# Tile 0 in smaller pieces, Fourier copies on ScalarE, and four moved steps between the stages of a diffusion layer

## The chip, the cores and the metric

The kernel runs on one core of one Trainium2 chip. The metric is the device time of one execution, in microseconds (us). All work is in float32, with matmuls whose operands are split into a high and a low part.

## What is computed

One layer of a diffusion backbone for 256 context tokens and 2048 latent tokens, width 1024. Cut to what matters:

```python
sh1, sc1, g1, sh2, sc2, g2 = split(silu(c) @ w_mod + b_mod, 6)      # modulation vectors, c_ctx for context tokens
h = rms_norm(x, norm1_g) * (1 + sc1) + sh1
q, k, v, f = project(h, w_in)                                        # QK-norm; rotary embedding on latent tokens
attn = diff_attention(q, k_all, v_all, lam)                          # (softmax_0 - lam * softmax_1) @ v, 4 heads
four = real(fft2(f, axes=(positions, channels))) @ w_four            # 4 groups of 128 channels
x = x + g1 * (concat[rms_norm(attn, subln_g) * (1 - lam_init), four] @ w_out)
h = rms_norm(x, norm2_g) * (1 + sc2) + sh2
x = x + g2 * (square(relu(h @ w1)) @ w2)
```

Outputs are x of both groups and the new keys and values of the context tokens.

## The kernel before

There are 18 tiles of 128 tokens. The stages follow each other: modulation vectors and tile 0, projections of all tiles, Fourier mixing, attention (4 heads, latent tokens in groups), the output projection, then the two layers of the MLP, each as a Strassen-like scheme of seven products per block (p is the product's number). A split matmul is three: high x high, low x high, high x low (`mm3`, lines 94 to 96). Most of the order is written out by hand in `manual_schedule` blocks; in attention a list of events sorted by a number sets it. Tiles of pools with `reuse_waits="tile"` share memory with those of earlier stages: a write waits until whatever lay at the address before is no longer read.

**Start (lines 471 to 590).** The modulation row is summed in two ways. Columns for `pr` go through TensorE (line 484); the rest is multiplied by VectorE into two accumulators, macc_l and macc_h (line 490), which VectorE reduces across partitions (line 528, `sums`), so that TensorE spreads them with the constant matrix `quad` (line 537, `pm`). Then scale and shift are made (modc, scale), tile 0's normalised and transposed x becomes hTa, its high and low parts hh and hl (lines 555, 556), and TensorE starts the projections `pj`. The weights arrive as `win`; ScalarE makes the high part wh (line 513), VectorE the low part wl (line 516).

**Fourier (lines 746 to 779).** `yT` makes for each item py and pz on TensorE (lines 753, 755); ScalarE copies py to yu; VectorE writes the difference and the sum of yu and pz to ys (lines 767, 768). Items are 512, 256, 128 and 129 (HW) columns wide; for the 512 wide ones pz is copied as well and the sums are made later. The result of each channel group, ys0 to ys3, is stored to DRAM (`four`) by a DMA that GpSimd issues (line 829).

**Attention.** TensorE makes scores Ss (line 1080), VectorE their maximum mxs, ScalarE the exponential into P0s or P1s (line 1104), GpSimd combines both (lines 1119, 1120), TensorE transposes into pts (line 1135), ScalarE or VectorE copies that to ahs (line 1142), VectorE makes the low part als (line 1147), and TensorE multiplies with V into po (lines 94 to 96, 1161). The outcome of a group goes through o1 to o6: o1 copies it to oTs, o2 transposes it back (line 1176), o3 is the VectorE copy to os (line 1180).

**Output projection (lines 1540 to 1720).** `out_mm(i, hf)` is 24 matmuls of a tile's half into po, `out_post` adds it to x on VectorE, `x_norm` makes xn, and `finish(i)` transposes xn in eight matmuls into two PSUM tiles ptb (line 248) from which ScalarE makes hTb in eight copies (line 251). `mix` transposes am (line 1572).

**MLP.** `h_parts(b, p)` returns two steps: `high` is ScalarE's copy mhh (line 1479), `rest` VectorE's mhl (line 1483). The weight sums are VectorE's: `mlp_ahead(2)` (line 1515) and `w_add` (line 1719, ws); oplW is the low part of a weight (line 1451). Products go to the PSUM tiles pA to pD, and VectorE takes them out as u and uz (lines 1771 to 1781). The second layer, the y stage, writes to six rotating PSUM tiles ps.

Of the kernel before, what the change touches and what calls it, by code (L numbers as in the profile page):

```python
# [37 lines left out]
def f32(ap):  # L38
    return ap.bitcast(F32)


def body(tc, a, out):
    nc = tc.nc
    ctx = ExitStack()
    with ctx:
# [211 lines left out]
        with ExitStack() as c1:  # L257
# [206 lines left out]
            with tc.manual_schedule():  # L464
                with tc.tile_pool(name="p0r", bufs=3) as rows, tc.tile_pool(name="p0m", bufs=KD - 3, side="right") as more:
# [8 lines left out]
                    z = quads(t2, "quad0")  # L474
# [7 lines left out]
                    for k in range(KD):  # L482
                        for gi, w in enumerate((512, 512, 256)):
                            nc.tensor.matmul(pr[gi][0:2, :w], cols[:, k:k + 9:8], wm[k][:, gi * 512:gi * 512 + w], start=(k == 0), stop=(k == KD - 1))
                        for s in range(2):
# [7 lines left out]
                        if 3 <= k < 7:  # L493
                            for x in (2 * k - 6, 2 * k - 5):
                                nc.tensor.transpose(at0(x), X[0][:, x * P:(x + 1) * P], ident)
                    X.pop(0)
# [4 lines left out]
                with tc.tile_pool(name="p0h", bufs=6, reuse_waits="tile") as halves:  # L501
# [24 lines left out]
                    sums = t2("sums0")[:, 0:48].rearrange("p (s c) -> p s c", s=2)  # L526
                    for s in range(2):
                        nc.vector.tensor_reduce(sums[:, s, :], acc[s].rearrange("p (c i) -> p c i", i=32), axis=AX.X, op=ALU.add,
                                                apply_transpose=True)
                    for gi in range(3):  # L530
                        w = 256 if gi == 2 else 512
                        r = t2(f"mr{gi}")
                        nc.scalar.copy(r[0:2, :w], pr[gi][0:2, :w])
                        for j in range(w // P):
                            nc.tensor.transpose(pm[:, gi * 4 + j, :], r[0:2, j * P:(j + 1) * P], ident[0:2, 0:2])
                    for q in range(4):
                        nc.tensor.matmul(pq, z[:, 96 - 32 * q:224 - 32 * q], sums[:, :, q::4], start=(q == 0), stop=(q == 3))
                    for g in range(4):
                        w_high(0, g)
                    w_rest(0, 0)  # L540
                    nc.vector.tensor_add(modc[:, 0:10, :], pm, cols[:, 32:42].unsqueeze(2).to_broadcast([P, 10, 2]))
                    nc.vector.tensor_add(modc[:, 10:16, :], pq.rearrange("p s j -> p j s"), cols[:, 42:48].unsqueeze(2).to_broadcast([P, 6, 2]))
                    mk_scale(scale1, 8, 80)
# [3 lines left out]
                    def h_first(b):  # L547
                        for k in range(4 * b, 4 * b + 4):
                            sc, sh, dst = scale1[:, k, 1:2], modc[:, k, 1:2], h0[b][:, k % 4, :]
                            if k in (2, 3):  # L550
# [3 lines left out]
                        hi, lo = (x[:, b * 4:b * 4 + 4, :] for x in HH[0])  # L554
                        nc.vector.tensor_copy(hi, h0[b])  # L555
                        nc.vector.tensor_sub(lo, h0[b], f32(hi))
# [1575 lines left out]
```

## Time and profile before

| | before |
|---|---|
| median of 3 runs | 2862.53 us (2861.9 to 2864.64) |
| profiled execution | 2863.18 us, span 2861.4 us |
| granted TensorE clock | 0.999 on average |
| TensorE busy | 2831.7 us, 99% of the span |
| VectorE, ScalarE, GpSimd busy | 71%, 54%, 38% |

Times in the profile count from the start of the span. "[1.56 <-DVE xn L235]" behind an instruction says that its engine stood idle for 1.56 us before it and that VectorE's xn ended that. PE is TensorE, PEld its weight loads, DVE VectorE, ACT ScalarE, POOL GpSimd. A matmul's duration contains the drain of its pipeline; distances between starts tell the pace.

### The profile page before, as it was taken

To read this page: it belongs to the slowest core of one execution; us is meant where nothing else is said; L and a number is where in the kernel's file an instruction comes from. 1 tells how busy PE (TensorE), PEld (TensorE's weight loads), DVE (VectorE), ACT (ScalarE), POOL (GpSimd) and SP (SyncE) were. 2 spreads that over 40 slices of the span, in tenths; PEclk is the share of its full clock that TensorE was granted. 3 is DMA by queue.
4 is the path that set the end of the run, shared out by engine and by line. 5 is a ranking of instruction groups with operands and counts; after the bars stand their busy time and mean duration, and the time that the engine had idled before them with its cause. 6 is when DMAs were issued, how large, how long until landed. Compare 5 with 4: busy or idle time off the path is not lost.

```text
span 2861.4 us, 43224 instructions
## 1 busy us (share of the span) xinstructions
PE 2831.7 (99%) x15109; PEld 2455.9 (86%) x15109; DVE 2018.0 (71%) x3393; ACT 1548.2 (54%) x3505; POOL 1073.3 (38%) x890
## 2 busy tenths in 40 slices
PE   8999999999999999999999999999999999999999
PEld 5888888688888888888889999999998888888887
DVE  7767886898988989864477777778775354345554
ACT  4333323798989989853356565556555332333221
POOL 1211223798999989942223333333332000000000
PEclk9999999999999999999999999999999999999999
DMA  7776777421211212036767676667747464445663
GB/s 284 219 207 198 230 213 237 172 106 38 73 71 53 106 38 99 23 124 201 242 221 232 223 246 228 221 219 238 234 167 255 147 202 135 138 144 185 206 206 111
DMA packets 392780, 492.94 MB, mean 172 GB/s; under 512 B 26467, under 2 KB 306384, under 8 KB 389490
## 3 DMA queue, kind: packets, MB, share of 16 engines
q1 hardware_dynamic: 387136, 479.73, 50.9%
q0 software_dynamic: 1872, 7.28, 0.8%
q10 hardware_dynamic: 3554, 3.17, 0.4%
q8 instruction: 119, 1.95, 0.3%
q14 instruction: 99, 0.81, 0.1%
HBM read 312.58 MB, written 179.59 MB: 172 GB/s over the span
## 4 chain that ended last, share of the span: by engine, by line
PE 54%; DVE 1%; DMA 0%; ACT 0%; issue 0%; SPq 0%; POOL 0%; DVEq 0%; POOLq 0%
PE ps L94 8%; PE ps L95 8%; PE ps L96 8%; PE pB L1749 2%; PE pB L1747 2%; PE pB L1748 2%; PE pA L1748 2%; PE pC L1748 2%; PE pA L1749 2%; PE pC L1747 2%; PE pA L1747 2%; PE pC L1749 2%; PE po L94 2%; PE po L96 2%; PE po L95 2%; PE pD L1749 1%
## 5 line engine op out<-in xcount | busy, mean ns | idle before, releaser
L1085 DVE TENSOR_REDUCE mxs<-Ss 128x1 f32<-128x512 f32 x636 | 405.4, 686 | 65.5 <-PE Ss L1080 55.1
L1420 DVE TENSOR_TENSOR sl<-sr,sh 128x768 fp32r<-128x768 f32 x168 | 161.8, 964 | 331.5 <-ACT sh L1419 331.1
L1120 POOL TENSOR_TENSOR P0s<-P0s,P1s 128x1024 f32<-128x1024 f32 (+2 forms) x128 | 378.6, 2958 | 10.7
L1419 ACT CAST sh<-sr 128x768 fp32r<-128x768 f32 x168 | 140.6, 838 | 418.3 <-PE ps L95 418.3
L1789 POOL TENSOR_TENSOR gs<-g,g 128x384 f32<-128x384 f32 x48 | 69.7, 1452 | 468.5 <-ACT g L1759 418.9
L1104 ACT ACTIVATE P1s<-Ss,mxs 128x512 f32<-128x512 f32 x318 | 215.4, 694 | 36.3 <-DVE mxs L1088 35.3
L94 PE MATMUL pj<-wh,hh 128*128 128x512 f32 x576 | 228.8, 397 | 2.0 <-DVE hh L555 2.0
L94 PE MATMUL ps<-thT,sh 128*128 128x512 f32 x585 | 227.6, 389 | 0.0
L95 PE MATMUL ps<-tlT,sh 128*128 128x512 f32 x585 | 227.6, 389 | 0.0
L96 PE MATMUL ps<-thT,sl 128*128 128x512 f32 x585 | 227.6, 389 | 0.0
L95 PE MATMUL pj<-wl,hh 128*128 128x512 f32 x576 | 227.1, 394 | 0.5 <-DVE wl L516 0.5
L96 PE MATMUL pj<-wh,hl 128*128 128x512 f32 x576 | 225.6, 392 | 0.0
L1104 ACT ACTIVATE P0s<-Ss,mxs 128x512 f32<-128x512 f32 x318 | 214.3, 691 | 5.6 <-DVE mxs L1088 5.0
L1135 PE MATMUL pts<-ident,P0s 128*128 128x128 f32 x1280 | 191.7, 273 | 4.5 <-DVE als L1147 1.8
L1080 PE MATMUL Ss<-KS0s,Qs 128*128 128x512 f32 x636 | 190.1, 419 | 0.4 <-ACT P1s L1104 0.4
L1080 PE MATMUL Ss<-KS1s,Qs 128*128 128x512 f32 x636 | 188.7, 420 | 1.5 <-ACT P0s L1104 1.4
L1758 ACT ACTIVATE g<-uz 128x384 f32<-128x384 f32 x144 | 75.7, 526 | 200.2 <-DVE uz L1781 174.1
L1135 PEld LDWEIGHTS pts<-ident,P0s 128*128 128x128 f32 x1280 | 151.3, 140 | 35.9 <-issue 4.8
L1119 POOL TENSOR_SCALAR P1s<-P1s,tots 128x1024 f32<-128x1024 f32 (+2 forms) x128 | 171.9, 1343 | 5.8
L1147 DVE TENSOR_TENSOR als<-pts,ahs 128x512 fp32r<-128x512 f32 x256 | 165.9, 681 | 6.9 <-ACT ahs L1142 6.7
L94 PE MATMUL ps<-ophT,sh 128*128 128x512 f32 x423 | 164.7, 389 | 1.1 <-DVE uz L1781 1.1
L96 PE MATMUL ps<-ophT,sl 128*128 128x512 f32 x423 | 164.6, 389 | 0.0
(536 smaller groups left out, 8073.9 us busy)
## 6 DMA issues: line engine op xcount, KB each, us to landing
sr<-sd SPq DMA_DIRECT2D x84, 768.0 KB, 4.5
a<-in_w SPq DMA_DIRECT2D x184, 256.0 KB, 4.2
sd<-gs SPq DMA_DIRECT2D x192, 192.0 KB, 1.9
sd<-g SPq DMA_DIRECT2D x144, 192.0 KB, 2.1
wm<-in_w_mod SPq DMA_DIRECT2D x32, 512.0 KB, 5.2
Qs<-qd SPq DMA_DIRECT2D x32, 512.0 KB, 4.0
b<-in_w SPq DMA_DIRECT2D x64, 256.0 KB, 5.8
b<-tsum SPq DMA_DIRECT2D x64, 256.0 KB, 4.7
```

Source lines behind the costliest of these rows:

```text
L94: nc.tensor.matmul(ps, lh, rh, start=first, stop=False)
L95: nc.tensor.matmul(ps, lh, rl, start=False, stop=False)
L96: nc.tensor.matmul(ps, ll, rh, start=False, stop=last)
L1080: nc.tensor.matmul(S[:, :w], self.Q[:, x, m, j * P:j * P + P], self.hd.KS[m][:, b * 512:b * 512 + w], start=(x == 0), stop=(x == 1))
L1085: nc.vector.tensor_reduce(self.mx[j][:, m, b:b + 1], self.S[j, m, b], axis=AX.X, op=ALU.max)
L1104: nc.scalar.activation(dst, S, AF.Exp, bias=self.mx[j][:, m, 6:7], accum_out=self.sm[j][:, m, b:b + 1])
L1119: nc.gpsimd.tensor_scalar(p, p, tot[:, 3:4], 0.0, op0=ALU.mult, op1=ALU.add)
L1120: nc.gpsimd.tensor_add(d, d, p)
L1135: nc.tensor.transpose(pt[:, c:c + P], self.p0[j][:, (kb + t) * P:(kb + t + 1) * P], ident)
L1747: nc.tensor.matmul(ps, wh[:, c], hh[:, k, :], start=first and k == 0, stop=False, skip_group_check=True)
L1748: nc.tensor.matmul(ps, wh[:, c], hl[:, k, :], start=False, stop=False, skip_group_check=True)
L1749: nc.tensor.matmul(ps, wl[:, c], hh[:, k, :], start=False, stop=k == 3, skip_group_check=True)
```

## The change

Six edits at six places. Lines of the changed kernel lie 13 to 20 higher.

1. Start: `quad` and `sums` go. TensorE multiplies each 128-column piece of the accumulators with a column of ones (12 matmuls into `pm`), macc_l is finished first, two transposes of x move behind, scale is made in two parts, and hh and hl of tile 0 in three pieces (columns 0 to 1, 2 to 3, 4 to 7); two of the weights' parts move ahead of modc.
2. Fourier: for items of 256 and 128 columns ScalarE copies pz too, into the second half of yu, which has four buffers in the stage's pool instead of two.
3. Attention: o3 of the last head's group 5 moves ahead in the list of events.
4. Output projection: `finish(s0)` moves behind `out_mm` of the third tile.
5. MLP: `mlp_ahead(2)` and `w_add(1, 0)` move behind `h_parts`.
6. y stage: three PSUM tiles are allocated ahead, which nothing uses.

```diff
@@ -471,7 +471,8 @@
         setup_cond(p1, pps, rw)
-        z = quads(t2, "quad0")
+        for n in range(2):
+            t2(f"place{n}")
         pr = [pp.tile([P, 512], F32, tag="pj", name=f"pr{gi}", bufs=4) for gi in range(3)]
@@ -482,7 +483,7 @@
                 nc.tensor.matmul(pr[gi][0:2, :w], cols[:, k:k + 9:8], wm[k][:, gi * 512:gi * 512 + w], start=(k == 0), stop=(k == KD - 1))
-            for s in range(2):
+            for s in (1, 0):
                 wk, sc = wm[k][:, 1280:2048], cols[:, 8 * s + k:8 * s + k + 1]
@@ -490,10 +491,9 @@
                 norm(p1, X[0], "a0")
-            if 3 <= k < 7:
+            if 3 <= k < 6:
                 for x in (2 * k - 6, 2 * k - 5):
                     nc.tensor.transpose(at0(x), X[0][:, x * P:(x + 1) * P], ident)
-        X.pop(0)
     wr = right.enter_context(tc.tile_pool(name="p1wr", bufs=1, side="right", reuse_waits="tile"))
@@ -523,39 +523,52 @@
         pq = pps.tile([P, 2, 6], F32, tag="pm", name="pm6")
-        sums = t2("sums0")[:, 0:48].rearrange("p (s c) -> p s c", s=2)
-        for s in range(2):
-            nc.vector.tensor_reduce(sums[:, s, :], acc[s].rearrange("p (c i) -> p c i", i=32), axis=AX.X, op=ALU.add,
-                                    apply_transpose=True)
+        w_high(0, 0)
+        w_rest(0, 0)
         for gi in range(3):
             w = 256 if gi == 2 else 512
             r = t2(f"mr{gi}")
             nc.scalar.copy(r[0:2, :w], pr[gi][0:2, :w])
+            if gi == 2:
+                for x in (6, 7):
+                    nc.tensor.transpose(at0(x), X[0][:, x * P:(x + 1) * P], ident)
+                X.pop(0)
             for j in range(w // P):
                 nc.tensor.transpose(pm[:, gi * 4 + j, :], r[0:2, j * P:(j + 1) * P], ident[0:2, 0:2])
-        for q in range(4):
-            nc.tensor.matmul(pq, z[:, 96 - 32 * q:224 - 32 * q], sums[:, :, q::4], start=(q == 0), stop=(q == 3))
-        for g in range(4):
-            w_high(0, g)
-        w_rest(0, 0)
-        nc.vector.tensor_add(modc[:, 0:10, :], pm, cols[:, 32:42].unsqueeze(2).to_broadcast([P, 10, 2]))
-        nc.vector.tensor_add(modc[:, 10:16, :], pq.rearrange("p s j -> p j s"), cols[:, 42:48].unsqueeze(2).to_broadcast([P, 6, 2]))
-        mk_scale(scale1, 8, 80)
+        for s in (1, 0):
+            for j in range(6):
+                nc.tensor.matmul(pq[:, s, j:j + 1], acc[s][:, j * P:j * P + P], ones, start=True, stop=True)
+        w_high(0, 1)
+        w_rest(0, 1)
         HH.update({i: tuple(p1.tile([P, KD, P], F32R, tag=f"h{x}", name=f"h{x}{i}") for x in "hl") for i in range(2)})
         h0 = [t2(f"hTa0_{b}").rearrange("p (k t) -> p k t", k=4) for b in range(2)]
-        def h_first(b):
-            for k in range(4 * b, 4 * b + 4):
-                sc, sh, dst = scale1[:, k, 1:2], modc[:, k, 1:2], h0[b][:, k % 4, :]
-                if k in (2, 3):
+        def h_pieces(ks):
+            for k in ks:
+                sc, sh, dst = scale1[:, k, 1:2], modc[:, k, 1:2], h0[k // 4][:, k % 4, :]
+                if k in (1, 3):
                     nc.vector.tensor_scalar(dst, at0(k), sc, sh, op0=ALU.mult, op1=ALU.add)
                 else:
                     nc.scalar.activation(dst, at0(k), AF.Identity, bias=sh, scale=sc)
-            hi, lo = (x[:, b * 4:b * 4 + 4, :] for x in HH[0])
-            nc.vector.tensor_copy(hi, h0[b])
-            nc.vector.tensor_sub(lo, h0[b], f32(hi))
-        h_first(0)
+            c, b = slice(ks[0], ks[-1] + 1), ks[0] // 4
+            src = h0[b][:, ks[0] % 4:ks[0] % 4 + len(ks), :]
+            hi, lo = (x[:, c, :] for x in HH[0])
+            nc.vector.tensor_copy(hi, src)
+            nc.vector.tensor_sub(lo, src, f32(hi))
+        def scale_part(c):
+            nc.vector.tensor_scalar_add(scale1[:, c, :], modc[:, 8 + c.start:8 + c.stop, :], 1.0)
+            nc.vector.tensor_mul(scale1[:, c, :], scale1[:, c, :],
+                                 cols[:, 80 + c.start:80 + c.stop].unsqueeze(2).to_broadcast([P, c.stop - c.start, 2]))
+        nc.vector.tensor_add(modc[:, 0:10, :], pm, cols[:, 32:42].unsqueeze(2).to_broadcast([P, 10, 2]))
+        scale_part(slice(0, 2))
+        h_pieces((0, 1))
+        nc.vector.tensor_add(modc[:, 10:16, :], pq.rearrange("p s j -> p j s"), cols[:, 42:48].unsqueeze(2).to_broadcast([P, 6, 2]))
+        scale_part(slice(2, KD))
+        for g in (2, 3):
+            w_high(0, g)
+        h_pieces((2, 3))
         norm_sq(p1, X[1], "a1")
@@ -564,12 +577,12 @@
                     w_high(k, g)
-                if k or g:
+                if k or g > 1:
                     w_rest(k, g)
             if k == 0:
                 norm_scale(X[1])
             if k == 1:
-                h_first(1)
+                h_pieces((4, 5, 6, 7))
                 load(2)
@@ -755,11 +768,15 @@
     late = w == 512
-    u, v = (yl if late else ft).tile([P, 512], F32, tag="yu", name="yu", bufs=4 if late else 2)[:, :w], pz[:, :w]
+    yu = (yl if late else ft).tile([P, 512], F32, tag="yu", name="yu", bufs=4)
+    u, v = yu[:, :w], pz[:, :w]
     nc.scalar.copy(u, py[:, :w])
     if late:
         v = yl.tile([P, 512], F32, tag="yv", name="yv", bufs=4)
         nc.scalar.copy(v, pz)
+    elif w != HW:
+        v = yu[:, 256:256 + w]
+        nc.scalar.copy(v, pz[:, :w])
@@ -1333,7 +1350,7 @@
         w = base + (AVS + 5) * T + 1.0 * u
-        for t, fn in ((0, gr.o1), (0.4, gr.o2), (0.75 if gr.last else 4.25, gr.o3), (8.5, gr.o4), (9.2, gr.o5), (9.6, gr.o6)):
+        for t, fn in ((0, gr.o1), (0.4, gr.o2), (0.75 if gr.last or h == H - 1 and g == 5 else 4.25, gr.o3), (8.5, gr.o4), (9.2, gr.o5), (9.6, gr.o6)):
             if gr.last and t:
@@ -1667,9 +1684,10 @@
     x_norm(s1)
-    finish(s0)
     for n, i in enumerate(seq[2:], 2):
         out_mm(i, 0)
+        if n == 2:
+            finish(s0)
         if n < N4 - 1:
@@ -1867,9 +1885,6 @@
         rest = None
-        if n == 3:
-            mlp_ahead(2)
-            w_add(1, 0)
         if n < 4:
@@ -1877,6 +1892,9 @@
                 h_load(0, ORDER[n + 5])
+        if n == 3:
+            mlp_ahead(2)
+            w_add(1, 0)
         if n == 5:
@@ -2016,6 +2034,8 @@
 with tc.manual_schedule():
+    for n in range(3):
+        pp.tile([P, 512], F32, tag="ps", name=f"place{n}", bufs=6)
     pend, NM, loaded, KS = None, 7 * 24, 4, []
```

What moves, as the two programs have it. First, ScalarE at the end of the Fourier stage and the start of attention (abl and yu are the last Fourier items, P0s the first exponentials of the first group, behind the bracket the semaphores waited on). Before:

```order
L810 COPY abl_0_5204<-pabl_0_5201 128x130 [waits PE_49]
L810 COPY abl_1_5209<-pabl_1_5206 128x130 [waits PE_49,Activation_49]
L759 COPY yu<-py 128x129 [waits PE_49] x2
L1104 ACTIVATE P0s_0_0_5294,sms_0_0_5271<-Ss_0_0_0_0_5273,mxs_0_0_5270 128x512 [waits DVE_49,Pool_49]
L1104 ACTIVATE P0s_0_0_5294,sms_0_0_5271<-Ss_0_0_0_1_5277,mxs_0_0_5270 128x512
```

In the change:

```order
L827 COPY abl_0_5218<-pabl_0_5215 128x130 [waits PE_49]
L827 COPY abl_1_5223<-pabl_1_5220 128x130 [waits PE_49,Activation_49]
L773 COPY yu<-py 128x129 [waits PE_49] x2
L1121 ACTIVATE P0s_0_0_5308,sms_0_0_5285<-Ss_0_0_0_0_5287,mxs_0_0_5284 128x512 [waits DMASW0_49,DVE_49,Pool_49]
L1121 ACTIVATE P0s_0_0_5308,sms_0_0_5285<-Ss_0_0_0_1_5291,mxs_0_0_5284 128x512
```

The first exponential has one wait more, DMASW0. It is a semaphore of the DMAs that GpSimd issues, and the value waited for is that of the store of ys3: with the larger yu buffers, ys3 lies 4096 bytes further up in each partition, and its end lies under this P0s.

Second, TensorE in the output projection at the third tile's first half (po_1_0 is its product, ptb the transposes of `finish`, the line with am is `mix`'s transpose). Before:

```order
L96 MATMUL po_9_0_15142<-woh_7_14925,ml_15015 128x512
L248 MATMUL ptb_0_15180<-ident,xn_15128 128x128 [waits DVE_49]
L248 MATMUL ptb_0_15180<-ident,xn_15128 128x128 x3
L248 MATMUL ptb_1_15189<-ident,xn_15128 128x128 x4
L94 MATMUL po_1_0_15198<-woh_0_14918,mh_15120 128x512
```

In the change:

```order
L96 MATMUL po_1_0_15193<-woh_7_14939,ml_15135 128x512
L248 MATMUL ptb_0_15219<-ident,xn_15142 128x128 [waits DVE_49]
L248 MATMUL ptb_0_15219<-ident,xn_15142 128x128 x3
L248 MATMUL ptb_1_15228<-ident,xn_15142 128x128 x4
L1589 MATMUL po<-ident,am_15150 128x128 [waits DMAHW0_49,Activation_49]
L1589 MATMUL po<-ident,am_15150 128x128 x3
L248 MATMUL ptb_0_15256<-ident,xn_15185 128x128 [waits DVE_49,Activation_49]
L248 MATMUL ptb_0_15256<-ident,xn_15185 128x128 x3
L248 MATMUL ptb_1_15265<-ident,xn_15185 128x128 [waits Activation_49]
L248 MATMUL ptb_1_15265<-ident,xn_15185 128x128 x3
L94 MATMUL po_1_1_15289<-woh_0_14948,mh_15134 128x512
```

The eight transposes of `finish(s0)` (ptb_0_15219, ptb_1_15228) now come behind po_1_0 and right ahead of the next tile's (ptb_0_15256, ptb_1_15265), which wait for ScalarE in both programs, since there are two such PSUM tiles.

Third, VectorE in the MLP's first products. Before:

```order
L1451 TENSOR_TENSOR oplW_4_17025<-a_0_16269,ophW_4_17024 128x512
L1515 TENSOR_TENSOR a_0_16265<-a_0_16265,wsa_16706 128x512
L1719 TENSOR_TENSOR ws_1_17041<-a_1_16714,a_1_16716 128x512
L1483 TENSOR_TENSOR mhl_4_17044<-hr_4_16976,mhh_4_17043 128x1536
L1719 TENSOR_TENSOR ws_1_17065<-ws_1_17041,a_1_16710 128x512
L1775 TENSOR_TENSOR u_0_17067<-pB_17001,us_16993 128x384
L1451 TENSOR_TENSOR oplW_1_17048<-a_1_16710,ophW_1_17047 128x512
```

In the change:

```order
L1468 TENSOR_TENSOR oplW_4_17039<-a_0_16283,ophW_4_17038 128x512
L1500 TENSOR_TENSOR mhl_4_17055<-hr_4_16990,mhh_4_17054 128x1536
L1532 TENSOR_TENSOR a_0_16279<-a_0_16279,wsa_16720 128x512
L1737 TENSOR_TENSOR ws_1_17059<-a_1_16728,a_1_16730 128x512
L1737 TENSOR_TENSOR ws_1_17079<-ws_1_17059,a_1_16724 128x512
L1793 TENSOR_TENSOR u_0_17081<-pB_17015,us_17007 128x384
L1468 TENSOR_TENSOR oplW_1_17062<-a_1_16724,ophW_1_17061 128x512
```

mhl_4 moved ahead of two subtractions (a, ws); the order of all others is as it was.

## Prediction

> **What bounds the kernel now.** I read the page first, then the waits of the whole span on TensorE, then the timeline around each place that the diff touches. The page's first section gives the engines' busy time:
>
> ```profile
> PE 2831.7 (99%) x15109; PEld 2455.9 (86%) x15109; DVE 2018.0 (71%) x3393; ACT 1548.2 (54%) x3505; POOL 1073.3 (38%) x890
> ```
>
> TensorE is busy for 2831.7 of 2861.4 us, so only its idle 29.7 us can be won without taking matmuls away. The waits on TensorE (us in total, times, longest) name the ones at which the diff aims:
>
> ```profile
> PE pj L94 <- DVE hh L555: 2.0, 1, 2.0
> PE ptb L248 <- DVE xn L235: 1.6, 1, 1.6
> PE pz L755 <- DVE ys L768: 1.4, 1, 1.4
> PE pD L1748 <- DVE mhl L1483: 1.1, 1, 1.1
> PE po L1161 <- DVE os L1180: 1.1, 2, 0.6
> PE ps L94 <- DVE uz L1781: 1.1, 1, 1.1
> ```
>
> Each part of the change has one row here. One of the two os waits (0.6) is touched. Together they are at most 7.8 us, 0.27% of the time. A few us of new waiting would eat that, so for each part I ask what is late next. About 0.2% (5.7 us) is what a measurement of this kernel tells from no change.
>
> **Fourier copies, and what they do to the first exponential.** For the eight 256 and 128 wide items ScalarE now also copies pz, and VectorE reads both parts from SBUF, so pz's bank no longer waits for a busy VectorE. The cost on ScalarE is four copies like each of these rows (ScalarE, 504 to 519, groups by form; count, busy, mean ns):
>
> ```profile
> L759 ACT COPY yu<-py 128x256 f32<-128x256 f32 x3 | 1.1, 373 | 0.1
> L759 ACT COPY yu<-py 128x128 f32<-128x128 f32 x4 | 1.1, 266 | 1.3 <-DVE ys L768 1.3
> ```
>
> For the narrow items that is four copies of 0.27 = 1.1 us an item, against 0.9 us of TensorE (eight matmuls of 128 columns; the eight at 1271.02 below take 1.09 with the drain of the last). So of the 1.4 won, up to 4 x 0.2 = 0.8 goes back: 0.6 to 1.4 stays, I take 1.0.
>
> But yu has four buffers instead of two, which moves ys3 up by 4 KB per partition, under the first attention group's P0s. The first exponential now waits for the store of ys3 to DRAM, too (the order rows above: DMASW0). Four such stores of 1 MB are issued on GpSimd, the first and last at
>
> ```profile
> 516.49 0.55 POOL L829 DMA_DIRECT2D four<-ys  x1 [5.55 <-DVE ys L768]
> 520.05 0.53 POOL L829 DMA_DIRECT2D four<-ys  x1 [0.35 <-issue]
> DMA to landing us min/median/max: 9.0/11.5/14.7
> ```
>
> and the third line, their time from issue to landing, puts the last landing at 520.05 + 14.7 = 534.75. In the stretch 521 to 535 the transfers read
>
> ```profile
> DMA packets 1308, 5.80 MB, mean 415 GB/s; under 512 B 148, under 2 KB 404, under 8 KB 795
> q0 software_dynamic: 576, 4.19, 71.1%
> ```
>
> That is the four stores (4.19 MB) and 1.6 MB of loads at a full rate. And before, the exponential and the TensorE matmul that needs its bank began at
>
> ```profile
> 522.70 0.69 ACT L1104 ACTIVATE P0s<-Ss,mxs 128x512 f32<-128x512 f32 x1 [4.04 <-DVE mxs L1088]
> 523.53 0.74 PE L1080 MATMUL Ss<-KS1s,Qs 128*128 128x512 f32 x2 [1.12 <-ACT P0s L1104]
> 524.00:534.00 10.00, 9.70 (x31) 4.23 (x29) 9.53 (x20) 9.75 (x31) 3.63 (x4) 1.00 1.02 420
> ```
>
> The last row (busy of PE, PEld, DVE, ACT, POOL in 524 to 534) has ScalarE at 9.75 of 10: it sets the pace of the attention's start, so what its first exponential loses, all behind it loses. If the stores start up to 1.4 earlier because the Fourier stage ends earlier, the last lands at 533.3 to 534.75; I take 534.0. The shift is 534.0 - 522.70 = 11.3 us, with the Fourier gain already inside. Bounds: 12.1 above; below, the stores' 4.19 MB alone at 415 GB/s from 519.6 end at 529.7, which is 7.0. Everything on ScalarE stands behind this wait (in order), TensorE fills its free banks and stops, VectorE and GpSimd follow. VectorE can meanwhile finish maxima, worth perhaps 0.5 later. Against that stands the clock after a stop of some 12 us. At the start of the program the stretches 31 to 35 and 35 to 38 read
>
> ```profile
> 31.00:35.00 4.00, 2.38 (x6) 1.86 (x7) 3.79 (x10) 3.88 (x9) 0.93 (x1) 0.50 0.82 334
> 35.00:38.00 3.00, 3.00 (x9) 2.38 (x8) 3.00 (x6) 3.00 (x8) 0.00 (x0) 0.55 0.88 294
> ```
>
> with a granted clock of 0.50 and 0.55 after an idle 2 us behind tiny matmuls. In the first of them six matmuls are busy for 2.38 us, 0.40 each. At that pace a tile's two take 0.8 us against ScalarE's 0.69 (row at 522.70), so for the 7 us ScalarE could wait 0.1 a tile, ten times: 0 to 1. I let the two cancel. The Trainium skill ("TensorE: Matmul & The Clock Gate", Part 1) has the clock halve after an idle activity window and return after about 3.4 us of sustained work; the 7 us here are two such windows.
>
> A rule of the Trainium skill speaks for a much smaller hold: "DMA: Bandwidth & Descriptors", section on the anatomy of a DMA on the gpsimd path, fits a transfer as 2.0 us plus bytes at 436 GB/s, by estimate 4.4 us for 1 MB. The rows above disagree: even the fastest of the four took 9.0 us, since they share a saturated path. What the fit would make of the time stands with the rivals.
>
> **finish(s0) behind out_mm(s2, 0).** Before, TensorE and (last row) ScalarE:
>
> ```profile
> 1269.07 0.39 PE L96 MATMUL po<-woh,ml 128*128 128x512 f32 x1
> 1271.02 1.09 PE L248 MATMUL ptb<-ident,xn 128*128 128x128 f32 x8 [1.56 <-DVE xn L235]
> 1277.45 0.60 PE L1572 MATMUL po<-ident,am 128*128 128x128 f32 x4
> 1278.68 0.48 PE L94 MATMUL po<-woh,mh 128*128 128x512 f32 x1
> 1273.43 2.89 ACT L251 ACTIVATE hTb<-ptb,modc,scale 128x128 f32<-128x128 f32 x8
> ```
>
> Before, the 24 matmuls of out_mm fill 1271.9 to 1277.45, 0.23 each. After, they run from 1269.3 to 1274.8, the eight transposes (0.11 each) to 1275.7, the four of am to 1276.1. Then come the eight of the next tile, and their two banks are those that hTb just filled: the first half waits for four of ScalarE's eight copies, the second for all. These start at 1275.4 (first four transposes done) and take 2.89, to 1278.3. The second half's four transposes (0.44) end the stage at 1278.75, where before it ended at 1278.68. So the 1.56 is given back within 7 us: +0.1, from -0.4 (ScalarE a little quicker) to +0.4. Before, the 24 matmuls stood between the two uses of these banks and hid the copies; that cover is moved away.
>
> **mlp_ahead and w_add behind h_parts.** Two VectorE subtractions move behind mhl:
>
> ```profile
> 1476.35 1.48 ACT L1479 CAST mhh<-hr 128x1536 fp32r<-128x1536 f32 x1 [2.24 <-DMA hr<-hd]
> 1476.38 0.69 DVE L1451 TENSOR_TENSOR oplW<-a,ophW 128x512 fp32r<-128x512 f32 x1
> 1476.99 0.69 DVE L1515 TENSOR_TENSOR a<-a,wsa 128x512 f32<-128x512 f32 x1
> 1478.19 1.76 DVE L1483 TENSOR_TENSOR mhl<-hr,mhh 128x1536 fp32r<-128x1536 f32 x1
> 1489.80 0.55 DVE L1771 TENSOR_TENSOR u<-pB,us 128x384 f32<-128x384 f32 x1
> 1490.40 0.19 PEld L1747 LDWEIGHTS pB<-mhh,ophW 128*128 128x128 f32 x1 [0.21 <-DVE u L1771]
> ```
>
> mhl reads mhh, which ScalarE ends at 1477.83 (it waited for a DMA). So mhl can start at 1477.86 instead of 1478.19: 0.33 won, not 1.1. VectorE's timeline shows no idle time over 0.03 from here to u at 1489.80; now it stands idle from 1476.99 to 1477.86, so all behind it is 0.87 later. TensorE's pB at 1490.40 waits for exactly that u (its bank). Net +0.9, from -0.3 (if the chain had slack) to +0.9.
>
> **o3 of the last head's group 5.** VectorE's and TensorE's rows:
>
> ```profile
> 1220.00 0.69 DVE L1142 COPY ahs<-pts 128x512 f32<-128x512 f32 x1 [0.26 <-PE pts L1135]
> 1224.10 0.42 DVE L1180 COPY os<-po 128x256 f32<-128x256 f32 x1
> 1220.41 0.44 PE L1176 MATMUL po<-ident,oTs 128*128 128x128 f32 x2 [0.44 <-ACT oTs L1172]
> 1220.68 1.04 PE L1135 MATMUL pts<-ident,P0s 128*128 128x128 f32 x8
> 1224.57 0.70 PE L1161 MATMUL po<-ahs,vf4s 128*128 128x256 f32 x2 [0.56 <-DVE os L1180]
> ```
>
> The os copy now precedes the ahs copy. It needs the two transposes that end at 1220.85, so os runs 1220.9 to 1221.3 and ahs to 1221.9 instead of 1220.69. The second four of the eight pts at 1220.68 (due at 1221.12) write the bank that ahs reads: they wait till 1221.95, 0.8 us, for 0.56 saved. Net +0.3, from -0.6 to +0.5.
>
> **place0 to place2 in the y stage.** No instruction touches these tiles, and the ps tiles have the same banks in both programs; the second, ps0_0_1, still lies on pC's bank and still waits for uz. The 1.1 stays: 0, with -1.1 at the far end.
>
> **Tile 0.** Rows of TensorE:
>
> ```profile
> 29.61 1.03 PE L537 MATMUL pm<-sums,quad 128*128 128x12 f32 x8 [0.17 <-DVE sums L528]
> 32.62 0.79 PE L94 MATMUL pj<-wh,hh 128*128 128x512 f32 x1 [1.98 <-DVE hh L555]
> 56.23 0.50 PE L95 MATMUL pj<-wl,hh 128*128 128x512 f32 x1 [0.47 <-DVE wl L516]
> ```
>
> The eight matmul records of L537 go (0.11 apart, 0.9 us); twelve matmuls on single columns come, 24 records, about 2.6 us. They end near 32.2, where hh's first two pieces are ready, so the first projection starts about 0.3 earlier. What VectorE and ScalarE do between is rearranged, not less. At 56.23 TensorE waits for the weights' low parts, so a lead of over 0.5 meets that wait, and the clock row above can move by a window either way. I take -0.5, from -2.0 to +0.9.
>
> **The sum.** -0.5 + 11.3 + 0.1 + 0.9 + 0.3 + 0 = +12.1. The profiled execution took 2863.18 us (span 2861.4), 0.65 above the median of 2862.53. So 2863.18 + 12.1 = 2875.3; I forecast 2875.
>
> **The rivals.** (a) Not slower: the last store is home when the first exponential comes. It decides at 522.7: a landing before costs nothing. Then -0.5 - 1.0 + 0.1 + 0.9 + 0.3 = -0.2, 2863. For it speaks only that the store may leave earlier; against it, 4.19 MB cannot pass in 2 us at 415 GB/s. Chance 0.08. A landing 4.4 us after the issue at 520.05 would leave a hold of 1.8 and 2866, which is in this chance; that is what the skill's fit would give. (b) All as meant: nothing is late next, and the store doesn't hold: the start's 0.5, then ys, xn, mhl, os and uz: -0.5 - 1.4 - 1.6 - 1.1 - 0.6 - 1.1 = -6.3, 2857. Chance 0.04. (c) The hold comes, but the moved steps pay as meant: 11.3 - 0.5 - 1.6 - 1.1 - 0.6 - 1.1 = +6.4, 2869.6. Chance 0.10. (d) The hold, and half clock without ScalarE's cover, or a slower drain of the stores: 12.1 + 1 to 4, up to 2879. Chance 0.08.
>
> **How the numbers follow.** The forecast keeps 0.70. The range 2869 to 2879 holds it, (c) and (d), with the bounds of the hold (7.0 to 12.1) and of the start; (a), (b) and some tails, under 0.2, lie outside. Faster by over 0.2% is (b), 0.04; within 0.2% is (a), 0.08; slower is the rest, 0.88.
>
> **What would show it.** In the profile after: a wait of the first ACT P0s on the DMA of four<-ys3, some 10 us longer than now, ending near 533 to 535, and TensorE's Ss wait grown from 1.1 to about 12; PE ptb waiting for ACT hTb; pD's wait down by 0.3 only and a new one of about 0.9 at pB; pts waiting for ahs near 1221; ps <- uz still 1.1. I am wrong if the first P0s starts within 2 us of its present place, or if the waits on xn, mhl, os and uz vanish with none beside them.

## The result and the profile after

The changed kernel takes 2880.09 us (median of four runs, 2877.22 to 2880.61) against 2862.62 for the kernel before, run beside it (four runs): a ratio of 1.0057, 95% interval 1.0044 to 1.007. It is slower by 17.5 us. The profiled execution took 2877.22 (span 2875.4), 14.0 above the profiled execution of before. First the page's engine line, then the waits on TensorE (us in total, times, longest) that answer to those shown of before:

```profile
PE 2836.9 (99%) x15125; PEld 2461.4 (86%) x15125; DVE 2020.2 (70%) x3395; ACT 1549.3 (54%) x3513; POOL 1071.8 (37%) x886
PE Ss L1097 <- ACT P0s L1121: 12.5, 3, 11.9
PE ptb L248 <- ACT hTb L251: 1.5, 2, 0.7
PE pabl L825 <- DVE s256s L854: 1.2, 1, 1.2
PE pD L1766 <- DVE mhl L1500: 1.1, 1, 1.1
PE ps L94 <- DVE uz L1799: 1.1, 1, 1.1
PE pts L1152 <- DVE ahs L1159: 0.9, 1, 0.9
PE pj L94 <- ACT wh L513: 0.8, 1, 0.8
PE pA L1767 <- DVE oplW L1468: 0.5, 1, 0.5
PE pB L1765 <- DVE u L1789: 0.3, 1, 0.3
```

Of the six waits that the prediction listed, hh, xn, ys and os are gone, mhl and uz stay, and hTb (1.5), s256s (1.2), ahs (0.9) and wh (0.8) stand in the places of those gone. The long one is new. In time order it is ScalarE's first exponential, the TensorE matmuls behind it, and the four stores on GpSimd that set it:

```profile
534.88 0.69 ACT L1121 ACTIVATE P0s<-Ss,mxs 128x512 f32<-128x512 f32 x1 [14.84 <-DMA four<-ys]
535.71 2.07 PE L1097 MATMUL Ss<-KS1s,Qs 128*128 128x512 f32 x4 [11.92 <-ACT P0s L1121]
517.86 0.55 POOL L846 DMA_DIRECT2D four<-ys  x1 [5.41 <-DVE ys L785]
521.43 0.53 POOL L846 DMA_DIRECT2D four<-ys  x1 [0.35 <-issue]
DMA to landing us min/median/max: 8.8/10.7/13.3
```

The last store is issued at 521.43 and lands 13.3 us later, at 534.77; the exponential starts 0.1 us after that, where it started at 522.70 before.

To see where time goes I subtract, for each VectorE and ScalarE instruction that two programs share, its start before from its start after, and take the median over a stretch of the program. The columns are stretches in the time of before; each row compares one profiled execution with that of before (the experiments follow below).

| kernel | tile 0 (64-80) | caches (445-500) | Fourier end (513-519) | attention (536-560) | behind o3, finish (1295-1440) | end (2300-2850) |
|---|---|---|---|---|---|---|
| changed | +3.1 | +1.3 | +1.4 | +12.9 | +12.7 | +14.1 |
| bufs_only | +0.6 | -0.3 | -0.2 | +13.5 | +13.1 | +13.2 |
| ys_apart | +1.9 | +0.7 | +0.9 | +4.0 | +4.0 | +5.6 |
| copies_apart | +0.5 | -1.4 | -1.3 | +2.9 | +3.7 | +3.7 |
| copies_apart_np | -0.3 | -0.8 | -2.5 | +1.1 | +1.7 | +1.6 |
| start_only | +1.8 | +0.8 | +0.8 | +0.8 | +0.7 | +0.7 |
| moves_only | -0.3 | -1.3 | -1.3 | -1.3 | -0.9 | -0.2 |
| all_but_copies | +2.6 | +1.5 | +1.5 | +1.4 | +1.8 | +3.1 |
| moves_softer | +0.8 | 0.0 | 0.0 | +1.0 | -0.7 | -1.4 |

Offsets ahead of an edit show how far single executions differ by themselves: up to 1.4 us by the caches in kernels of the table that are unchanged up to there, and 2.2 in moves_copies. Steps between two columns are the readings. In bufs_only and moves_softer the offset steps inside 536-560, near 547, from +12.4 to +13.5 and from 0.0 to +1.0; the table has the value behind the step, and the last section shows what it is.

### The profile page after: what moved, and what is told of

It is laid out like the page before. It is cut to its first block, busy times and chain, and to the rows that moved or that the text cites. A ratio compares the mean times of both kernels' runs of the same rounds, so it can differ in the third digit from the quotient of the medians.

```text
span 2875.4 us, 43247 instructions
## 1 busy us (share of the span) xinstructions
PE 2836.9 (99%) x15125; PEld 2461.4 (86%) x15125; DVE 2020.2 (70%) x3395; ACT 1549.3 (54%) x3513; POOL 1071.8 (37%) x886
## 4 chain that ended last, share of the span: by engine, by line
PE 93%; DMA 2%; DVE 2%; ACT 1%; POOL 1%; issue 0%; SPq 0%; ACTq 0%; POOLq 0%; DVEq 0%
PE Ss L1097 10%; PE ps L94 8%; PE ps L96 8%; PE ps L95 8%; PE pts L1152 5%; PE pj L95 4%; PE pj L96 4%; PE pj L94 4%; PE po L96 4%; PE po L94 4%; PE po L95 4%; PE pB L1765 2%; PE pB L1767 2%; PE pB L1766 2%; PE pA L1766 2%; PE pC L1765 2%
## 5 line engine op out<-in xcount | busy, mean ns | idle before, releaser
L95 PE MATMUL ps<-oplT,sh 128*128 128x512 f32 x423 | 164.6, 389 | 0.0
```

Of the source, the lines that this page charges most:

```text
L95: nc.tensor.matmul(ps, lh, rl, start=False, stop=False)
```

## The experiments

Kernels are built on the kernel before unless said otherwise. Three groups were run together, each with its own runs of the kernel before: bufs_only, ys_apart, start_only and moves_only (before: 2862.20 us, 22 runs); copies_two_bufs, copies_no_pool, start_wl_first and moves_softer (2863.07, 33 runs); copies_apart, copies_apart_np, moves_copies and all_but_copies (2863.37, 33 runs).

**bufs_only: the larger buffers without the copies.**

```diff
-bufs=4 if late else 2)[:, :w], pz[:, :w]
+bufs=4)[:, :w], pz[:, :w]
```

> The kernel before with one number changed: four yu buffers in the Fourier stage's pool instead of two, no copy of pz. Theory (the moved ys3 holds the first exponential): +11 to +12.5 us, about 2874.5; the first P0s waits for the DMA of four<-ys3 until about 534.8, and TensorE's wait for ys of 1.4 us before pz stays. Rival (the copies or ScalarE's extra work cause the hold, not the address): within 1 us of before, and the first P0s stays at 522.7.

Measured: 2876.71 us (2876.34 to 2876.94), ratio 1.0051 (1.0034 to 1.0068). ScalarE's and TensorE's waits between 495 and 560 us:

```profile
ACT P0s L1104 <- DMA four<-ys: 16.1, 1, 16.1
PE Ss L1080 <- ACT P0s L1104: 13.4, 2, 13.2
```

No instruction was added; ys3 lies 4096 bytes higher, under P0s, and that alone gives the hold: the last store landed at 534.43 and the first exponential started at 534.53.

**ys_apart: the changed kernel with the narrow yu in a pool of its own,** so that ys3 stays clear of P0s.

```diff
-yu = (yl if late else ft).tile([P, 512], F32, tag="yu", name="yu", bufs=4)
+yu = (yl if late else yn).tile([P, 512], F32, tag="yu", name="yu", bufs=4)
```

> The changed kernel, with the four narrow yu buffers in a pool of their own behind the others, so that ys3 does not lie under the first P0s. All six edits remain. Theory: the hold of 11.3 us goes; what is left against before is the start +2.9, Fourier -1.5 and the moves +1.3, so 2.7 us over before in the profile (2866) and 11 to 12 us under the changed kernel. Rival (the attention's start is limited by the stores' traffic anyway, or a later tile waits for them): less than 6 us come back.

Measured: 2871.22 us (2868.01 to 2872.89), ratio 1.0029 (1.0018 to 1.0040). That is 8.9 us less than the changed kernel, where 11 to 12 were expected. The exponential is no longer held, but another wait stands 12 us behind it (Qs are the queries of the attention):

```profile
PE Ss L1098 <- DMA Qs<-qd: 3.5, 1, 3.5
```

Nothing in the prediction had this wait; it made the copies suspect (below).

**start_only and moves_only: tile 0's edit alone, and the four moved places alone** (the hunks of the diff ahead of that in yT, and those behind it).

> The kernel before with the edit of tile 0 alone. Theory (the second weight request goes out 2 us later, because the low part that frees its buffer now stands behind the second modc, and all requests after it follow): +2.5 to +3.5 us in the profile, about 2866, made before 62 us; that request at 37.2 instead of 35.2. Rival, as predicted: -0.5 us, 2862. If the 2 to 3 us by which the changed kernel's other executions exceed its profiled one arise here, executions of this kernel spread as widely.

> The kernel before with the edits 3 to 6 alone (o3, finish, mlp_ahead and w_add, the unused tiles), without tile 0 and the Fourier copies. Theory: o3 +0.3, finish +0.1, mlp +0.9, unused tiles 0: +1.3 us, about 2864. Rival, each step pays what its wait showed: -0.6 - 1.6 - 1.1 - 1.1 = -4.4 us, 2858.

Measured: 2864.15 us (2862.73 to 2866.86) for the start and 2864.06 (2862.61 to 2867.94) for the moves, both with ratio 1.0007 (0.9998 to 1.0016). Each is about 1.9 us above before by the medians, and neither can be told from no change alone. For the start this lies between the theory (+2.5 to +3.5) and its rival (-0.5) and settles neither; for the moves the theory (+1.3) fits and the rival (-4.4) is out. In the offsets the start loses 1.8 by 64-80 and ends at +0.7; the moves lose 0.4 at o3 and finish, 0.7 at the MLP and nothing at the y stage.

**copies_two_bufs and copies_no_pool: the copies, with no tile moved.** In the first all narrow pieces get the copy of pz, with two yu; the second leaves out those 256-column pieces that run beside GpSimd's work.

```diff
+elif w != HW:                          # copies_two_bufs
+elif w == 128 or w == 256 and g == 3:  # copies_no_pool
+    v = yu[:, 256:256 + w]
+    nc.scalar.copy(v, pz[:, :w])
```

> The kernel before with the Fourier copies alone: the narrow yu keeps its two buffers, so no tile changes its address, and pz is copied into the second half of yu. Theory 1 (what ate the gain is what VectorE and GpSimd share): in the traces so far a subtraction ys<-yu of 128x256 with both operands in SBUF takes 1.09 to 1.69 us while GpSimd runs its own ys and yd, and 0.61 us behind it; with one operand in PSUM it took 0.62 to 0.65 us beside the same work. Six to eight such instructions come before s256s and s256d, so s256d ends some 3 us later than in the kernel before (about 513.3 instead of 510.3), TensorE waits 1 to 1.3 us for s256s instead of 1.4 us for ys, and the load of Vs, which waits for s256d, goes out at 513.3 instead of 510.4. Then the stage itself ends within 0.3 us of the kernel before, the loads are caught among the four stores, the first query load behind them arrives late, and TensorE waits some 3 us for Qs about 535: 2864.5 to 2866. Theory 2 (the prediction's own reckoning): the copies free pz early and pay 1.0 to 1.4 us: 2861. Theory 3 (the late loads came with the other edits, not with the copies): Vs goes out at 510 and the time is 2861 to 2862.5.

> The copies of pz only where GpSimd is about to be done: for the pieces of 128 columns and, of the pieces of 256, for the last group alone; the other 256-column pieces keep one operand in PSUM as in the kernel before. Theory 1: the six subtractions and additions beside GpSimd's work stay at 0.62 to 0.65 us, s256d ends at 510.3 as before, Vs is requested at 510.4, and pz of the last group is free early, so TensorE's wait of 1.4 us for ys at 511.4 goes: all behind it comes 1.0 to 1.4 us earlier, 2861 to 2861.5. Theory 2 (the copies cost as such, whatever lies beside them): Vs late as in the kernel with all copies, 2864 or more. No effect on the hold of the stores by either: their tiles stay where they are.

Measured: 2866.01 us (2864.68 to 2874.26), ratio 1.0013 (1.0004 to 1.0022), and 2864.40 (2862.70 to 2868.80), ratio 1.0006 (0.9997 to 1.0014). The first came out at the upper end of theory 1 (TensorE's wait for Qs was 2.1 us). The second missed: TensorE's 1.44 us only changed its name, since with two yu ScalarE's next copy waited for VectorE to be done with the buffer. Since two buffers add a wait of their own, the pair was repeated with four.

**copies_apart and copies_apart_np: the same pair with four yu in a pool of their own.**

```diff
+yn = c2.enter_context(tc.tile_pool(name="f_n", bufs=4, reuse_waits="tile"))
+yu = (yl if late else yn).tile([P, 512], F32, tag="yu", name="yu", bufs=4)
```

> The kernel before with all of the Fourier copies, and four narrow yu in a pool of their own, so that no later tile lies on another's address. Theory 1 (SBUF operands beside GpSimd): the six ys<-yu ahead of s256s take 1.1 to 1.7 us each, s256d ends at 512.5 to 513.5 instead of 510.3, the load of Vs goes out at 512.5 to 513.5, TensorE waits about 1.2 us for s256s and 2 to 3.5 us for Qs near 535: 2 to 3.5 us above the kernel before. Rival (the lateness in the earlier run came from having two buffers alone): s256d on time, the wait of 1.4 us for ys gone, 1.0 to 1.4 us below the kernel before.

> The same with the copies only for the 128-column pieces and the last 256-column piece; this and the run beside it differ in nothing but where the second operand of the other 256-column pieces lies. Theory 1: the six instructions ahead of s256s stay at 0.62 to 0.65 us, s256d ends at 510.3, Vs is requested at 510.4, no wait for Qs. With four buffers ScalarE frees pz of the last group at once, which two buffers did not allow (there ScalarE's copy waited 1.9 us for ys and TensorE's 1.44 us stayed): the wait of 1.4 us at 511.4 goes or shrinks to what s256d leaves (0 to 0.4 us), and the end comes 0.5 to 1.4 us earlier than in the kernel before. Rival (copies into SBUF cost whatever lies beside them, or the stores that set the end of the stage do not move): 0 to +1 us.

Measured: 2867.27 us (2865.97 to 2869.72), ratio 1.0014 (1.0005 to 1.0023), and 2864.03 (2862.01 to 2865.70), ratio 1.0002 (0.9993 to 1.0011); no run of the first was as short as the longest of the second. VectorE and GpSimd side by side in copies_apart (start, us):

```profile
505.95 0.98 POOL L780 TENSOR_TENSOR ys<-yd 128x256 f32<-128x256 f32 x1
506.31 1.12 DVE L772 TENSOR_TENSOR ys<-yu 128x256 f32<-128x256 f32 x1
508.80 0.98 POOL L783 TENSOR_TENSOR ys<-yu 128x256 f32<-128x256 f32 x1
509.16 1.09 DVE L773 TENSOR_TENSOR ys<-yu 128x256 f32<-128x256 f32 x1
510.10 0.68 DVE L842 TENSOR_TENSOR s256s<-ss 128x512 f32<-128x512 f32 x1
511.29 0.61 DVE L772 TENSOR_TENSOR ys<-yu 128x256 f32<-128x256 f32 x1
```

and in copies_apart_np (each POOL row is what GpSimd was at when the VectorE rows behind it began, up to the last, which began alone):

```profile
503.69 1.46 POOL L777 TENSOR_TENSOR yd<-yu,yv 128x512 f32<-128x512 f32 x1
503.93 0.62 DVE L772 TENSOR_TENSOR ys<-yu,pz 128x256 f32<-128x256 f32 x1
504.86 0.65 DVE L772 TENSOR_TENSOR ys<-yu,pz 128x256 f32<-128x256 f32 x1
507.15 0.73 POOL L781 TENSOR_TENSOR ys<-yd 128x256 f32<-128x256 f32 x1
507.33 1.10 DVE L842 TENSOR_TENSOR s256s<-ss 128x512 f32<-128x512 f32 x1
508.98 1.18 POOL L783 TENSOR_TENSOR ys<-yu 128x256 f32<-128x256 f32 x1
509.49 1.16 DVE L772 TENSOR_TENSOR ys<-yu 128x256 f32<-128x256 f32 x1
510.49 0.62 DVE L773 TENSOR_TENSOR ys<-yu 128x256 f32<-128x256 f32 x1
```

The same instruction takes 1.1 us while GpSimd works and 0.61 behind it, and 0.62 to 0.65 beside GpSimd when one operand is in PSUM. s256s, the sum that TensorE's pabl needs, has both operands in SBUF and shows it the other way: 1.10 beside GpSimd, 0.68 behind. The Trainium skill ("SBUF — State Buffer", section "SBUF: two separate sides") states it: GpSimd's port pair is one of VectorE's, and a VectorE instruction with two SBUF inputs and a GpSimd instruction that reads SBUF shut each other out. The rows agree: each ys<-yu shown beside GpSimd ends 0.47 to 0.50 us after the GpSimd instruction that it met (506.93 and 507.43, 509.78 and 510.25, 510.16 and 510.65), so most of it runs only when GpSimd is done.

Without that loss the copies pay as meant: in copies_apart_np the step at the Fourier stage is -1.7 us (-0.8 to -2.5). It is then given back, 3.6 us by 536-560, to a wait that copies_apart has too. In both, SyncE's request of vf14s (a load of 128 KB for the attention), GpSimd's first of the four stores, that load's time to land, and the next wait on TensorE read (copies_apart, then copies_apart_np, then the request and the landing for before):

```profile
512.25 0.46 SPq L1039 DMA_DIRECT2D vf14s<-vs  x1
515.18 0.55 POOL L834 DMA_DIRECT2D four<-ys  x1 [5.41 <-DVE ys L773]
DMA to landing us min/median/max: 21.0/21.0/21.0
534.51 2.53 PE L1085 MATMUL Ss<-KS0s,Qs 128*128 128x512 f32 x6 [4.18 <-DMA Qs<-qd]
```

```profile
510.44 0.46 SPq L1039 DMA_DIRECT2D vf14s<-vs  x1
513.99 0.56 POOL L834 DMA_DIRECT2D four<-ys  x1 [3.83 <-DVE ys L773]
DMA to landing us min/median/max: 20.6/20.6/20.6
532.28 2.90 PE L1085 MATMUL Ss<-KS0s,Qs 128*128 128x512 f32 x6 [3.17 <-DMA Qs<-qd]
```

```profile
511.22 0.46 SPq L1034 DMA_DIRECT2D vf14s<-vs  x1
DMA to landing us min/median/max: 9.9/9.9/9.9
```

Before, the first store is asked for at 516.49, 5.3 us behind that load, and the load lands after 9.9 us. With a lead of 2.9 to 3.6 us (4.7 in copies_two_bufs) it lands some 21 us after its request, about when the last store does, and the query load behind it comes too late. In copies_apart the lead is short because the load is asked for 1.0 us later than before, in copies_apart_np because the stores are 2.5 us earlier. In the eight kernels here with a lead of 5.3 us there is no such wait. The DMA's view of the kernel before, 518 to 521 and then 521 to 528, says what the lead buys:

```profile
DMA packets 659, 0.68 MB, mean 228 GB/s; under 512 B 48, under 2 KB 560, under 8 KB 658
q0 software_dynamic: 328, 2.42, 81.9%
q1 hardware_dynamic: 378, 0.48, 19.7%
```

The stores (q0) move their first packet at 521.1, 4.6 us after the first of them is asked for, and by then 560 small packets of the loads (q1) are through. From then on both queues move packets in like numbers, but a store's packet is of 7.4 KB and a load's of 1.3, so the loads get 0.48 MB in 7 us. In copies_two_bufs 525 small packets were through before the first of the stores, in copies_apart, copies_apart_np and moves_copies no more than 31. So an earlier end of the Fourier stage was worth nothing here: its stores then meet the attention's loads.

**start_wl_first: tile 0's edit alone, with the low halves of two weight pieces put back in front** (the code shortened, against the changed kernel).

```diff
+for g in (2, 3):
+    w_high(0, g)
+    w_rest(0, g)
 nc.vector.tensor_add(modc[:, 10:16, :], ...)
 scale_part(slice(2, KD))
-for g in (2, 3):
-    w_high(0, g)
```

> The start of the changed kernel in the kernel before, with one thing put back: VectorE makes the low halves of the third and fourth weight piece of the first row block (wl_0_2, wl_0_3) ahead of the second modulation sum, so that the weight buffers come free, and the next loads are asked for, about as early as in the kernel before. Theory 1 (the loss of the start is the weight requests that went out 2 us late): the second request goes out at 34 to 35.5 instead of 36.8, ScalarE's and TensorE's waits for weights near 58 shrink, and the offset against the kernel before at 64 to 80 us falls from +1.8 to between -0.5 and +0.6: 2861.5 to 2862.5. Rival (the loss comes from TensorE's later first projection, half a clock longer, and the pieces of tile 0 themselves): the requests go out earlier, but the offset at 64 to 80 stays at +1.2 or more and the time at 2863.5 to 2864.5.

Measured: 2864.02 us (2861.97 to 2864.67), ratio 1.0003 (0.9994 to 1.0012). The next weight request goes out at 34.14 us instead of 36.82 in start_only, but the one behind it only at 39.10 (38.65), and the offset at 64-80 is +1.2. That is the rival's figure: earlier requests alone do not take the loss away. But the edit also moves ScalarE's high halves, and puts the second modc at 34.03 instead of 33.12 (start_only), so what the order alone costs stays open.

**moves_softer and moves_copies: other places for o3, finish and the y stage; the second also with copies_apart_np** (shortened).

```diff
-0.75 if gr.last else 4.25, gr.o3
+0.75 if gr.last else 2.5 if h == H - 1 and g == 5 else 4.25, gr.o3
-finish(s0)
+if n == 2: out_mm(i, 0, 0, 3); finish(s0); out_mm(i, 0, 3)
+if ... or (i, b, k) == (0, 0, 0): continue      # the first k waits for the second
-for j in range(3):
+for j in (0, 2, 1) if (i, b, k) == (0, 0, 1) else range(3):
```

> The kernel before with three of the moved places set otherwise than in the changed kernel: o3 of the last attention group at 2.5 instead of 4.25 or 0.75 units (behind the copy of ahs and ahead of the totals), finish(s0) behind the first three steps of the next output product instead of before it or behind all of it, and the first step of the y stage in the order 0, 2, 1 with its first k deferred. Theory (each of these places has a wait of its own in the kernel before that other matmuls can cover: pts for os about 0.9, ptb for xn 1.6, pD for mhl 1.1): some 0.6 us at o3, 1.5 at finish and 1.1 at the y stage, together 2 to 3.2 us: 2859 to 2860.5. Rival (the waits only change their releaser, as they did in the changed kernel, or what follows is bound by loads): 2861.5 to 2863.

> The last kernel and the softer moves of o3, finish and the y stage together. Theory: the gains lie in different stages and add: the moves alone were 2.3 us below the kernel before, the copies are expected at 0.5 to 1.4 us, together 2.8 to 3.7 us below. Rival: the Fourier stage's gain is given back to the loads ahead of the attention, 2.0 to 2.5 us below.

Measured: 2860.78 us (2859.49 to 2862.07), ratio 0.9992 (0.9983 to 1.0001), and 2860.80 (2859.00 to 2862.76), ratio 0.9993 (0.9984 to 1.0001). Both medians are 2.3 and 2.6 us below before, with intervals that just reach no change. By the offsets of moves_softer finish gains 1.8 us, the y stage 0.7 and o3 nothing. No wait of ptb is left between 1215 and 1300 (one of po for os still takes 1.3), and the one at uz reads

```profile
PE ps L94 <- DVE uz L1785: 0.3, 1, 0.3
```

instead of 1.1. Adding the copies brings nothing, as the rival of moves_copies had it: vf14s, with a lead of 3.6 us, landed 19.7 us after its request, and TensorE waited 2.4 us at 530 (the profile names ScalarE's P1s, not Qs, as what ended it).

**all_but_copies: the changed kernel without its Fourier edit** (every hunk of the diff but that in yT).

> The changed kernel without its Fourier copies: tile 0 and the four moved places as they are, yu, pz and ys as in the kernel before. Theory (the parts add): the hold of the first exponential is gone, the start costs what it cost alone (0.7 us by the offset behind the caches, 1.9 us by the medians) and the moved places what they cost alone (1.6 us by the offsets, 1.9 us by the medians): 2.3 to 3.8 us above the kernel before. Rival (the late start pushes the stores or the loads into a new wait, so that part of the changed kernel's loss is not the copies'): 6 us or more above.

Measured: 2866.63 us (2864.95 to 2869.00), ratio 1.0012 (1.0003 to 1.0021): 3.3 us above before, as the parts' sum said. So the Fourier edit accounts for some 14 of the 17.5 us.

## Why the prediction was right, and where it was not

It forecast slower, by the hold of the first exponential, and that is what happened. The median, 2880.1, is 5 us above the forecast and 1.1 above the top of the range; the profiled execution gained 14.0 where the sum had 12.1. Term by term, in that execution:

- **The hold.** Forecast: the last store lands at 534.0 and the exponential starts 11.3 later, Fourier gain inside, with -0.5 of the start ahead of it. Measured: landing 534.77, exponential 12.2 later, of which 1.4 was there already at the Fourier stage's end; so the hold itself is 10.8, and 11.5 by 536-560. The mechanism, the buffer's address and the drain of the stores were right, and bufs_only shows the address alone doing it.
- **The Fourier gain.** Forecast 1.0 inside the hold. Measured -0.1 (offset +1.3 to +1.4): none. The step that failed is "VectorE reads both parts from SBUF" taken as free. Those reads collide with GpSimd's, s256s comes later, and TensorE waits 1.2 us for it instead of 1.4 for ys. Under the hold this was hidden, as was the late load of vf14s (18.7 us); with the hold taken away it costs 3.9 us (copies_apart, medians). The rule of the Trainium skill quoted above would have said so beforehand, and I did not weigh it.
- **The clock after the stop.** Forecast: 0 to 1, cancelled against VectorE's head start. The windows (granted clock is third from the right) read

```profile
528.00:536.00 8.00, 0.29 (x1) 0.29 (x2) 0.00 (x0) 1.12 (x3) 0.00 (x0) 0.50 1.01 410
538.00:540.00 2.00, 2.00 (x6) 1.60 (x5) 1.80 (x4) 1.53 (x5) 0.00 (x0) 0.50 0.00 0
540.00:544.00 4.00, 3.65 (x13) 2.08 (x12) 3.77 (x10) 3.70 (x13) 0.82 (x3) 0.92 0.01 2
```

  Behind the store's landing the clock stays at half until about 540, and the offset grows by 0.7 (10.8 to 11.5); nothing cancelled it.
- **Tile 0.** Forecast -0.5; measured +3.1 at 64-80, of which +1.3 is left behind the cache stage. (Most of the rest is given back at 310 us, where TensorE waits 0.9 for a load of the cache in the kernel before and not in the changed one; moves_only, which has none of this edit, gains 0.7 at the same place.) The step that failed is the twelve single-column products ending near 32.2. The last row is that of start_only, the others are of the changed kernel:

```profile
30.04 1.50 PE L540 MATMUL pm<-ones,macc_l 128*128 128x1 f32 x12
31.41 2.11 PE L540 MATMUL pm<-ones,macc_h 128*128 128x1 f32 x12
33.37 0.77 PE L94 MATMUL pj<-wh,hh 128*128 128x512 f32 x1
33.55 0.17 DVE L567 TENSOR_TENSOR modc<-pm,cols 128x12 f32<-128x12 f32 x1 [0.75 <-PE pm L540]
35.90 1.28 DVE L516 TENSOR_TENSOR wl<-win,wh 128x512 fp32r<-128x512 f32 x2
31.60 1.48 PE L540 MATMUL pm<-ones,macc_h 128*128 128x1 f32 x12
```

  They started 0.4 late, since the two transposes of x now stand ahead of them, took 3.5 us instead of 2.6 and ended at 33.5; the first projection came 0.75 later, not 0.3 earlier. Some 0.6 of that is the clock: it was 0.50 from 32.1 to 33.5, where the last records are 0.21 apart instead of 0.11. In start_only it stayed at 1.00, they ended at 33.08, and the first projection still came 0.3 later than before. VectorE waits for them, and the next two low halves of the weights follow at 35.90 (33.27 before). The rest of VectorE's list comes about 2 us later. start_wl_first shows that putting two of these back in front isn't enough.
- **finish, o3.** Forecast +0.1 and +0.3; the offsets give +0.05 for both (+0.4 to +0.8 in moves_only, by where one starts to count, all of it at o3). hTb took xn's place and pts waits 0.9 for ahs, as forecast.
- **The MLP.** Forecast +0.9 with new waits at pB; measured +1.3 here and +0.7 in moves_only, with 0.3 at pB and 0.5 at pA, which was not foreseen. pD's wait stayed at 1.1: mhh, which waits for a load (hr), started at 1489.40, 0.33 later than the offset alone puts it, and that is the whole gain forecast. In moves_only mhh came 0.3 earlier, and pD's wait fell to 0.5.
- **place0 to place2.** Forecast 0, measured 0: ps still waits 1.1 for uz.

The sum of the parts by medians is 14.5 + 1.9 + 1.9 = 18.3 for bufs_only, start_only and moves_only, near the 17.5 measured. What lies between the profiled execution and the others of the changed kernel goes with the clock: the profiled one ran at a mean of 0.996 and took 2877.2, the other three at 0.995 and took 2879.7 to 2880.6. In ys_apart three runs at 0.998 took 2868.0 to 2869.0 and four at 0.996 took 2871.2 to 2872.9. Where in the program that clock is lost has no profile, and stays open. Rival (d), at a chance of 0.08, had 1 to 4 us for such a loss, and the median lies 1.1 above even that: the mechanism of the hold was right, the size of what goes with it was put too low.

## What to carry to other kernels

Before a buffer count is raised, look at what its pool pushes to another address, and which transfer still reads there: here 4 KB cost 14.5 us (bufs_only), and the copies that needed the buffers gained 1.7 us at best (copies_apart_np, ahead of the wait for Qs). An operand that moves from PSUM to SBUF is not free on VectorE while GpSimd works: look at what runs beside it. And a stage that ends earlier starts its stores earlier; before counting the gain, see which loads are still on the way and how small their packets are.

## What the runs showed of the hardware

- A VectorE subtraction of 128x256 with two SBUF operands took 1.1 us (1.69 beside GpSimd's 512-column ones) against 0.61 alone; with one operand in PSUM it took 0.62 to 0.65 beside the same work.
- A load of 128 KB asked for 4.7 us or less ahead of 4 MB of stores landed 18.6 to 21.0 us after its request (six kernels); with a lead of 5.3 us it landed after 9.7 to 10.3 (eight kernels). Each is one profiled execution. What goes with it is whether the loads' small packets are through before the stores' first, which came 4.6 us after their issue in the kernel before (560 there, 525 in copies_two_bufs at 4.7); a test that changes the lead alone is missing.
- The same idle time can cost half the clock or not. In moves_softer, behind a wait of 1.37 us at 543.8 (1.38 before), TensorE ran at 0.50 where it ran at 1.00 before, 1.0 us by the next wait. The step of bufs_only in the table is the same (a wait of 1.36 at 556.3, then a clock of 0.50 from 556.8 to 560.2):

```profile
544.00:546.00 2.00, 2.00 (x8) 1.71 (x8) 0.28 (x2) 2.00 (x7) 1.92 (x2) 0.50 0.00 0
544.00:546.00 2.00, 1.69 (x9) 1.18 (x9) 1.06 (x3) 2.00 (x7) 1.92 (x2) 1.00 0.00 0
```

The first row is moves_softer, the second before.
